# A 4 KB descriptor ring, one more place in five buffers, and two mixer norms moved in a decoder step's program

## The chip, the cores and the metric

The kernel runs on one core of a Trainium2 chip. A core has five engines that run side by side, each with its own queue of instructions: TensorE (PE, matrix products; PEld is its weight load), VectorE (DVE), ScalarE (ACT), GpSimd (POOL) and SyncE (SP, which here only starts transfers). They meet through semaphores. Transfers between the memory of the chip and the core's SBUF run on 16 DMA engines and are started from SP's, ACT's and POOL's queues. The metric is the device time of one execution in microseconds.

## The reference

One layer of a decoder for 512 prompt tokens and 8 x 8 sample tokens, width 2048, in float32.

```python
mod = (silu(c) @ w_ada + b_ada).reshape(-1, 6, D)        # shift1, scale1, gate1, shift2, scale2, gate2
h = rmsnorm(x) * (1 + scale1) + shift1
x_lru, y_gate, sc_b, sc_c, sc_x = split(h @ w_in)        # five groups of 1024 columns
out_lru = rglru(conv4(x_lru)) * gelu(y_gate)             # a recurrence over the tokens
out_sc = sc_b * conv3(sc_c * sc_x)
x = x + gate1 * (concat([rmsnorm(out_lru), rmsnorm(out_sc)]) @ w_out)
h2 = rmsnorm(x) * (1 + scale2) + shift2
# PEER: 8 heads, each takes the 16 best of 128 x 128 experts for each token
act = gelu(h2 . u[e]) * softmax(score)                   # for each token and chosen expert e
x = x + gate2 * sum(act * v[e])
y = rmsnorm(x)
```

Beside y, the last states of the recurrence and of both convolutions are returned. The inputs scale some of the norm weights and biases up.

## The kernel before

Products are made to float32 accuracy from three reduced ones: each operand is split into a high part (ACT's cast) and a low part (a subtraction on POOL or DVE), and TensorE adds high x high, low x high and high x low. A block of weights therefore passes SP's load (`raw`), ACT (`hi`), POOL (`lo`) and TensorE, in that order, through a few rotating places.

**Phase 1** (to about 960 us) has all 576 tokens in the free dimension. The order of TensorE's work is the order of the program text; that of the other engines is the scheduler's. The modulation is 96 pieces of 1 MB of `w_ada`, loaded into the pool `adap` (line 161). 32 of them run at the start; the other 64 stand in the list `todo` (line 349) and are put between the projections by `ada_turn(n, keep=7)` (line 351), which issues at most n pieces, stops at the end of a group of four, and leaves `keep` of them in the list. Lines 553 to 570 project and run the recurrence, eight tiles of 128 channels; lines 574 to 588 the short convolution, three projections (c, s, b) for each of eight tiles with `ada_turn(2)` behind each. `norm_stats` (line 224) puts a sum of squares through TensorE and takes a reciprocal root on DVE; the function that it returns, `spread` (line 232), has TensorE copy the root to all partitions and ACT copy that out to a buffer `R`. The recurrence's output is scaled by it inside the first short-conv tile (lines 578 to 586). The short convolution's is scaled at lines 597 to 604, between the first halves of the first two output tiles (`out_half`) and their second halves. Behind the output projection come gate, residual, second norm and queries.

**Phase 2** has two long stages in a hand-written order for all engines (line 985). Blocks of 128 experts with one first key are ranked by how many tokens choose them. The L = 80 first are computed densely, for all 512 prompt tokens, by products with whole blocks of u and v. The rest, and all sample tokens, are fetched as rows: a gather on POOL (`take`, line 1202) brings one expert's row for each of 128 partitions, and DVE multiplies and sums it.

- **U stage**, lines 1611 to 1682, 160 half-blocks n: `ahead` (line 910) loads and converts u's blocks, `u_half` (line 1363) runs 24 matmuls. Between them go the gate weights of the dense blocks, four tokens at a time: `g_pair` (DVE builds one-hots), `g_scale` (ACT scales them), `g_mm` (TensorE, into one PSUM bank) and `g_out` (ACT copies the bank to `stg`). `gm` holds how many groups have been built, multiplied and scaled. `LAG` holds the multiplication back by so many half-blocks, `PAIRS` bounds how many groups stand between building and multiplying, and PAIRS // 2 is the number of their buffers. The gathered rows of u go through `RB` places (`new_row`, line 827), fetched RB - 1 ahead (line 1304).
- **V stage**, lines 1722 to 1752, 80 steps m of two 512 KB blocks of v: `ahead(n + 7, n + 3)` loads seven blocks ahead and converts three ahead. `v_column` (line 1381) runs 12 matmuls for one of four PSUM banks, and `v_sum` (line 1410) adds a finished bank to the result on DVE, which frees it. The rows of v go through `RV` places, fetched RV - 2 ahead. Raw blocks have four places: two in the pool `ws`, one in `wx`, one in `vx`, taken in turn by `load` (line 880).

DVE and POOL serve several of these at once, in order: POOL holds the gathers and the subtractions in one queue, DVE the row products, the one-hots and the sums.

Of the kernel before, what the change touches and what calls it, by code (L numbers as in the profile page):

```python
# [39 lines left out]
SORTED = ((0, 64, 34), (64, 128, 47), (192, 128, 37), (320, 128, 30), (448, 64, 11))  # L40
RB = 4
RV = 6
ENDS = 5
# [6 lines left out]
FULL_ROWS = 1.25  # L50
LAG = 3
FIRST_G = 6
PAIRS = 6
EARLY_V = 16
# [26 lines left out]
def build(ctx, tc, A, O, dbg=None):  # L81
    nc = tc.nc
# [77 lines left out]
    big = p1.enter_context(tc.tile_pool(name="big", bufs=1))  # L160
    adap = p1.enter_context(tc.tile_pool(name="adap", bufs=3))
    wk = p1.enter_context(tc.tile_pool(name="wk", bufs=1))
# [188 lines left out]
    def ada_turn(n, keep=7):  # L351

        for a in pend:
            ada_out(*a)
        pend.clear()
        for _ in range(min(n, len(todo) - keep)):
            a = todo.pop(0)
            ada_mm(*a)
            if a[2] == 3:
                pend.append(a[:2])  # L360
                break
# [212 lines left out]
    for i in range(KW):  # L574
        sc_c(i, project(A["w_in"][24 + i], f"c{i}") if i else pc0)
        ada_turn(2)
        sc_x(i, project(A["w_in"][32 + i], f"s{i}"))
        if i == 0:
            spread = norm_stats(st, W, "g0")
        ada_turn(2)  # L580
        if i == 0:
            R = spread()
            st = []
            for k in range(KW):
                V.scalar_tensor_tensor(o[:, k, :], o[:, k, :], cols[:, C_GN + k:C_GN + k + 1], R, op0=ALU.mult, op1=ALU.mult)
        sc_b(i, project(A["w_in"][16 + i], f"b{i}"))
        ada_turn(2)
        square_sum(o[:, KW + i, :], i, st, "g1")
# [9 lines left out]
    spread = norm_stats(st, W, "g1")  # L598
    out_half(1, 0)
    ada_turn(2)  # L600
    R = spread()
    for k in range(KW, KD):
# [32 lines left out]
    R = spread()  # L635
# [244 lines left out]
    def load(n):  # L880
        if n >= len(stream):
            return
        s = stream[n]
        k = n % 3 if n < NU2 + 2 else (n - NU2 - 2) % 4
        pool, b = (ws, 2) if k < 2 else (wx, 1) if k == 2 else (pools["vx"], 1)
        raw = pool.tile([128, 8, 128], F32, name=f"raw{n}", tag="wraw", bufs=b)
# [710 lines left out]
    R1 = R2 = None  # L1597
    gm = [0, 0, 0, 0]
    ep = None
# [11 lines left out]
    for n in range(NU2):  # L1611
# [7 lines left out]
        if R1 is not None:  # L1619
# [8 lines left out]
            while gm[2] < gm[3]:  # L1628
                g_scale(gm[2])
                gm[2] += 1  # L1630
            gm[3] = gm[0]

# [89 lines left out]
    for m in range(M):  # L1722
        gi, q, bl, first, final = steps[m]
        n = NU2 + 2 * m
        ahead(n + 3, n + 3)
        ahead(n + 7, n + 3)
        if m == last:
# [181 lines left out]
```

## Time and profile before

| | |
|---|---|
| timed runs | 3267.7, 3271.77, 3271.31 us, median 3271.31 |
| profiled execution | 3275.15 us, its span 3273.3 us |
| granted TensorE clock, mean | 0.976 |
| moved by DMA | 882.84 MB |
| first matmul with u, first with v | about 1201 and 2262 us |

The timed runs differ by 0.12%. The profile is of one execution, 3.84 us above the median. Its page gives busy time for each engine, a chain of the work that ended last, and groups of instructions by line. Windows give the same for stretches of the span, waits say which engine stood idle and what ended the idle time, and a timeline lists instructions in order. A row of a timeline has start, length, engine, line, operation, the tiles written and read, and in brackets the idle time before it with what ended it. A row of waits has the total, how many times, and the longest.

### The profile page before, as it was taken

To read this page: it belongs to the slowest core of one execution; us is meant where nothing else is said; L and a number is where in the kernel's file an instruction comes from. 1 tells how busy PE (TensorE), PEld (TensorE's weight loads), DVE (VectorE), ACT (ScalarE), POOL (GpSimd) and SP (SyncE) were. 2 spreads that over 40 slices of the span, in tenths; PEclk is the share of its full clock that TensorE was granted. 3 is DMA by queue.
4 is the path that set the end of the run, shared out by engine and by line. 5 is a ranking of instruction groups with operands and counts; after the bars stand their busy time and mean duration, and the time that the engine had idled before them with its cause. 6 is when DMAs were issued, how large, how long until landed. Compare 5 with 4: busy or idle time off the path is not lost.

```text
span 3273.3 us, 46692 instructions
## 1 busy us (share of the span) xinstructions
PE 3088.6 (94%) x17239; PEld 2616.8 (80%) x17239; DVE 2173.3 (66%) x3265; ACT 1056.9 (32%) x1645; POOL 1718.4 (52%) x1000
## 2 busy tenths in 40 slices
PE   5999999999989999999999998998999999989897
PEld 2788898889979998887788787886888777777686
DVE  3465521142246898897998979856777787978755
ACT  3244311132232222222665555542222121122122
POOL 2233233344343335666556655656777676777742
PEclk9999999999989999999999999998999999999998
DMA  9744466634342228989779898989999988998964
GB/s 375 266 144 136 163 221 203 214 99 146 131 140 67 72 90 277 308 310 381 312 297 405 340 369 315 395 285 385 389 372 387 391 327 315 344 365 305 369 218 163
DMA packets 297067, 882.84 MB, mean 270 GB/s; under 512 B 37590, under 2 KB 79446, under 8 KB 245366
## 3 DMA queue, kind: packets, MB, share of 16 engines
q1 hardware_dynamic: 160608, 380.39, 33.3%
q0 software_dynamic: 66336, 413.41, 32.1%
q10 hardware_dynamic: 69888, 86.00, 7.5%
q8 instruction: 136, 2.23, 0.3%
q14 instruction: 99, 0.81, 0.1%
HBM read 879.89 MB, written 66.81 MB: 289 GB/s over the span
## 4 chain that ended last, share of the span: by engine, by line
PE 67%; DMA 15%; DVE 7%; issue 4%; POOL 4%; ACT 2%; ACTq 0%; SPq 0%; POOLq 0%; DVEq 0%
PE pu L1373 19%; PE pv L1393 14%; PE pp_o L139 6%; DMA v<-v,rows 4%; DMA gsb<-gd 4%; PE pp_c L139 3%; PE pp_s L139 3%; PE qa L139 3%; PE pp_b L139 3%; PE qb L139 3%; PE gbank L1573 2%; PE pp_x L139 2%; PE pp_y L139 2%; PE ada L189 2%; POOL xlo L905 2%
## 5 line engine op out<-in xcount | busy, mean ns | idle before, releaser
L905 POOL TENSOR_TENSOR xlo<-raw,xhi 128x1024 fp32r<-128x1024 f32 x320 | 785.6, 2467 | 453.8 <-ACT xhi L904 440.5
L904 ACT ACTIVATE xhi<-raw 128x1024 fp32r<-128x1024 f32 x320 | 338.2, 1060 | 868.6 <-PE pv L1393 353.6
L1258 DVE SCALAR_TENSOR_TENSOR accB<-v,dots,accB 128x2048 f32<-128x2048 f32 x211 | 496.3, 2352 | 159.4 <-DMA v<-v,rows 154.0
L1231 DVE SCALAR_TENSOR_TENSOR u<-u,hT 128x2048 f32<-128x2048 f32 x223 | 505.0, 2282 | 145.1 <-DMA u<-u,rows 130.2
L1393 PE MATMUL pv<-ahi,xhi 128*128 128x512 f32 x1280 | 514.8, 402 | 43.7 <-DVE acc L1415 33.7
L1393 PE MATMUL pv<-ahi,xlo 128*128 128x512 f32 x1280 | 510.8, 399 | 10.7 <-POOL xlo L905 10.5
L1373 PE MATMUL pu<-hhi,xhi 128*128 128x512 f32 x1280 | 516.9, 404 | 1.6 <-ACT xhi L904 1.6
L1373 PE MATMUL pu<-hhi,xlo 128*128 128x512 f32 x1280 | 504.7, 394 | 6.5 <-POOL xlo L905 6.5
L1393 PE MATMUL pv<-alo,xhi 128*128 128x512 f32 x1280 | 507.7, 397 | 0.0
L1373 PE MATMUL pu<-hlo,xhi 128*128 128x512 f32 x1280 | 506.0, 395 | 0.0
L1203 POOL DMA_INDIRECT u<-u,rows x223 | 227.6, 1021 | 207.1 <-DVE u L1231 155.2
L1393 PEld LDWEIGHTS pv<-ahi,xhi 128*128 128x128 f32 x1280 | 244.3, 191 | 107.8 <-DVE acc L1415 24.8
L1393 PEld LDWEIGHTS pv<-ahi,xlo 128*128 128x128 f32 x1280 | 244.1, 191 | 72.1 <-POOL xlo L905 15.1
L1203 POOL DMA_INDIRECT v<-v,rows x223 | 260.4, 1168 | 77.9 <-issue 36.3
L1373 PEld LDWEIGHTS pu<-hhi,xlo 128*128 128x128 f32 x1280 | 242.7, 190 | 61.7 <-POOL xlo L905 7.4
L1393 PEld LDWEIGHTS pv<-alo,xhi 128*128 128x128 f32 x1280 | 244.6, 191 | 54.7
L1373 PEld LDWEIGHTS pu<-hhi,xhi 128*128 128x128 f32 x1280 | 243.3, 190 | 52.5 <-ACT xhi L904 2.1
L1373 PEld LDWEIGHTS pu<-hlo,xhi 128*128 128x128 f32 x1280 | 243.0, 190 | 47.8
L1567 ACT ACTIVATE op<-op,it 128x128 f32<-128x128 f32 x512 | 155.9, 389 | 82.5 <-DVE op L1559 82.5
L1573 PEld LDWEIGHTS gbank<-wr,op 128*128 128x128 f32 x1024 | 134.4, 193 | 42.5 <-ACT stg L1580 33.1
L1573 PE MATMUL gbank<-wr,op 128*128 128x80 f32 x1024 | 133.6, 274 | 25.7 <-ACT stg L1580 25.5
L128 POOL TENSOR_TENSOR wlo_q<-raw_q,whi_q 128x1024 fp32r<-128x1024 f32 x28 | 67.8, 2420 | 142.5 <-ACT whi_q L126 142.5
(481 smaller groups left out, 5452.2 us busy)
## 6 DMA issues: line engine op xcount, KB each, us to landing
wa<-w_ada SPq DMA_DIRECT2D x96, 1024.0 KB
raw<-ut SPq DMA_DIRECT2D x160, 512.0 KB
raw<-v SPq DMA_DIRECT2D x320, 256.0 KB
actd<-act ACTq DMA_DIRECT2D x80, 256.0 KB
gd<-stg ACTq DMA_DIRECT2D x64, 320.0 KB
gsb<-gd ACTq DMA_DIRECT2D x80, 256.0 KB
actr<-actd ACTq DMA_DIRECT2D x40, 512.0 KB
raw_o<-w_out SPq DMA_DIRECT2D x32, 512.0 KB
```

The source lines that it names most:

```text
L128: lo_engine(share).tensor_sub(lo, raw, r32(hi))
L139: PE.matmul(o, st, mv[pick](k), start=first, stop=last)
L189: PE.matmul(acc[32 * g:32 * g + 32, :], cpad[:, 4 * kq + g, :], w[:, g, :], start=kq == 0, stop=kq == 3)
L904: S.activation(hi, raw, AF.Copy)
L905: G.tensor_sub(lo, raw, r32(hi))
L1203: G.indirect_dma_start(out=out, out_offset=None, in_=src, in_offset=bass.IndirectOffsetOnAxis(ap=idx, axis=0), bounds_check=NE * 128 - 1, ...
L1231: V.scalar_tensor_tensor(r, r, 1.0, st["h"], op0=ALU.mult, op1=ALU.mult, accum_out=dots[i][:, j:j + 1])
L1258: V.scalar_tensor_tensor(st["a"], r, dots[i][:, j:j + 1], st["a"], op0=ALU.mult, op1=ALU.add)
L1373: PE.matmul(pu, st[:, kk, :], movA[mv](k), start=k == 0 and a == 0, stop=k == KD - 1 and a == 2)
L1393: PE.matmul(pv, st, mv, start=first and j == 0 and a == 0, stop=last and not end and j == SG - 1 and a == 2)
L1567: S.activation(ops[:, j0 + j, :], ops[:, j0 + j, :], AF.Copy, scale=it[2][:, b * 4 + j:b * 4 + j + 1])
L1573: PE.matmul(pg[:, j * L:(j + 1) * L], ops[:, j0 + j, :], wr[:, j0 + j, :], start=True, stop=True)
```

## The change

[...] LAG grows by one and the list `gm` by one entry, so that a group is scaled one half-block later than before. In phase 1 the first `spread` is called behind the projection of the b tile and DVE's scalings behind `sc_b`; the second is called ahead of `ada_turn(2)`, and a second `ada_turn(2)` follows.

```diff
-RB = 4
-RV = 6
+RB = 5
+RV = 7
-LAG = 3
+LAG = 4
-PAIRS = 6
+PAIRS = 8
-    adap = p1.enter_context(tc.tile_pool(name="adap", bufs=3))
+    adap = p1.enter_context(tc.tile_pool(name="adap", bufs=4))
...
         ada_turn(2)
+        pb_ = project(A["w_in"][16 + i], f"b{i}")
         if i == 0:
             R = spread()
             st = []
+        sc_b(i, pb_)
+        if i == 0:
             for k in range(KW):
                 V.scalar_tensor_tensor(o[:, k, :], o[:, k, :], cols[:, C_GN + k:C_GN + k + 1], R, op0=ALU.mult, op1=ALU.mult)
-        sc_b(i, project(A["w_in"][16 + i], f"b{i}"))
         ada_turn(2)
...
     out_half(1, 0)
+    R = spread()
     ada_turn(2)
-    R = spread()
+    ada_turn(2)
     for k in range(KW, KD):
...
-        k = n % 3 if n < NU2 + 2 else (n - NU2 - 2) % 4
-        pool, b = (ws, 2) if k < 2 else (wx, 1) if k == 2 else (pools["vx"], 1)
+        k = n % 3 if n < NU2 + 2 else (n - NU2 - 2) % 5
+        pool, b = (ws, 2) if k < 2 else (wx, 1) if k == 2 else (pools["vx"], 2)
...
-    gm = [0, 0, 0, 0]
+    gm = [0, 0, 0, 0, 0]
...
-            gm[3] = gm[0]
+            gm[3], gm[4] = gm[4], gm[0]
...
-        ahead(n + 7, n + 3)
+        ahead(n + 8, n + 3)
...
-    nc = _bacc.Bacc("TRN2", target_bir_lowering=False, num_devices=1)
+    nc = _bacc.Bacc("TRN2", target_bir_lowering=False, num_devices=1, dynamic_dma_scratch_size=4096)
```

## The prediction

> **What bounds the kernel now.** I read the page first, then the windows, then the waits, then the timeline of the places that the change touches. The page:
>
> ```profile
> PE 3088.6 (94%) x17239; PEld 2616.8 (80%) x17239; DVE 2173.3 (66%) x3265; ACT 1056.9 (32%) x1645; POOL 1718.4 (52%) x1000
> PE 67%; DMA 15%; DVE 7%; issue 4%; POOL 4%; ACT 2%; ACTq 0%; SPq 0%; POOLq 0%; DVEq 0%
> ```
>
> TensorE is busy 94% of the span and holds 67% of the chain that ended last. No edit takes a matmul away, so only time that TensorE loses can be won. The busy share hides part of that time, because matmuls that follow a stall run slower. I therefore count matmuls. The next three rows are 25 us windows of TensorE alone; their columns are length, busy time (instructions), granted clock, DMA share, GB/s.
>
> ```profile
> 2350.00:2375.00 25.00, 25.00 (x110) 1.00 1.04 394
> 2575.00:2600.00 25.00, 19.47 (x70) 0.86 0.95 359
> 2075.00:2100.00 25.00, 25.00 (x135) 1.00 1.02 424
> ```
>
> Undisturbed, the V stage starts 110 matmuls in 25 us (4.4 per us); the U stage, with the small gate matmuls between, 135 (5.4 per us). The window at 2575 lost 40 matmuls, 9.1 us, although only 5.5 us of it were idle. With these rates I price whole stretches (all engines: PE, PEld, DVE, ACT, POOL, then clock, DMA share, GB/s):
>
> ```profile
> 0.00:135.00 135.00, 95.61 (x613) 54.42 (x613) 46.65 (x108) 40.96 (x67) 37.52 (x37) 0.91 0.96 357
> 1600.00:1850.00 250.00, 238.96 (x1239) 200.42 (x1238) 221.44 (x289) 148.50 (x323) 150.97 (x104) 0.99 0.93 372
> 1850.00:2100.00 250.00, 236.12 (x1217) 199.88 (x1216) 216.06 (x275) 143.53 (x312) 146.12 (x100) 0.97 0.88 340
> 2275.00:2575.00 300.00, 299.02 (x1289) 242.39 (x1287) 222.59 (x128) 73.46 (x74) 209.13 (x123) 1.00 1.01 385
> 2575.00:2875.00 300.00, 277.54 (x1152) 220.56 (x1152) 243.55 (x138) 63.21 (x58) 210.73 (x127) 0.97 0.90 338
> 2875.00:3175.00 300.00, 277.78 (x1178) 221.76 (x1179) 221.13 (x137) 64.05 (x59) 200.65 (x117) 0.98 0.85 309
> ```
>
> U loses (1350 - 1239)/5.4 = 20.6 us and (1350 - 1217)/5.4 = 24.6 us in its two rows, 45 us. V loses (1320 - 1289)/4.4 = 7, then 38 and 32 us: 77 us, 70 of them after 2575. What TensorE waited for, over the whole run:
>
> ```profile
> PE ada L189 <- DMA wa<-w_ada: 36.4, 15, 18.2
> PE pv L1393 <- DVE acc L1415: 33.7, 18, 4.9
> PE gbank L1573 <- ACT stg L1580: 25.5, 15, 5.6
> ACT op L1567 <- DVE op L1559: 82.5, 37, 11.5
> ```
>
> **V stage: one more row place, fetch depth 4 to 5, one more raw place.** One disturbance, POOL, ACT and DVE timelines merged in order of time:
>
> ```profile
> 2571.87 1.06 ACT L904 ACTIVATE xhi<-raw 128x1024 fp32r<-128x1024 f32 x1 [12.92 <-DMA raw<-v]
> 2573.02 4.15 POOL L905 TENSOR_TENSOR xlo<-raw,xhi 128x1024 fp32r<-128x1024 f32 x1 [7.73 <-ACT xhi L904]
> 2580.67 1.00 POOL L1203 DMA_INDIRECT v<-v,rows  x1
> 2589.33 2.36 DVE L1258 SCALAR_TENSOR_TENSOR accB<-v,dots,accB 128x2048 f32<-128x2048 f32 x1 [9.72 <-DMA v<-v,rows]
> ```
>
> A raw block is late, ACT waits 12.92 us, POOL waits behind ACT, the gathers queued behind POOL's subtraction go out late, and DVE then waits 9.72 us for a row. DVE's sums (L1415) free TensorE's PSUM banks, so TensorE stops too: that is the 33.7 us above. The waits of 2575 to 3175 alone, and the gathers of 2275 to 3180:
>
> ```profile
> ACT xhi L904 <- DMA raw<-v: 115.6, 27, 21.2
> DVE accB L1258 <- DMA v<-v,rows: 78.9, 38, 10.0
> L1203 POOL DMA_INDIRECT v<-v,rows x207: 987/998/3089, 2274.0 to 3126.8; - x104
> ```
>
> A mean row wait is 78.9/38 = 2.1 us, a mean raw wait 115.6/27 = 4.3 us. One more row of lead is 852.8/207 = 4.1 us; one more raw block is 24 matmuls, 24/4.4 = 5.5 us. So each added place is worth more than the mean wait it stands against, less than the longest (10.0 and 21.2). The bounds: nothing, if the transfers simply end later; at most 70 us after 2575. DMA leaves room for it: (0.90 + 0.85) x 300 = 525 us of DMA work at the share of 1.01 that the row of 2275 holds is 520 us, and TensorE needs (1152 + 1178)/4.4 = 530 us for these 600. But both floors are nearly equal, and in stretches where DMA is full an added place is used once and not refilled, so I take 40% of the 70: **28 us** (range 10 to 50).
>
> **U stage: fifth row, LAG 4, PAIRS 8, the scale one half-block later.** The gate bank is one PSUM bank: TensorE's next group waits until ACT has copied it out (25.5 us in 15 waits). ACT is late because its scaling of the one-hots stands in its queue ahead of the copy and waits for DVE: 82.5 us in 37 waits, 2.2 us each, longest 11.5. The longer gm list moves each scaling one half-block back, which is 24 + 16 matmuls, 40/5.4 = 7.4 us. That covers all but the longest of these waits. LAG and PAIRS keep the matmul one step and one buffer behind, so nothing is taken back. What is not covered is ACT's wait at a change of token group:
>
> ```profile
> L1218 ACT ACTIVATE hT<-h2r 128x2048 f32<-128x2048 f32 x5 | 9.5, 1903 | 13.3 <-DVE u L1231 12.1 <-DMA h2r<-h2d,tok 1.2
> ```
>
> Of the 94.6 us that ACT waits for DVE (82.5 + 12.1), 87% go, so 22 of the 25.5; DVE itself is busy 216 to 221 us of 250 and catches up slowly, so I take not quite two thirds of that, **14 us**, between nothing and the 45 counted. The fifth row shortens DVE's waits for rows, but as the window at 2075 shows a DMA share of 1.02 in this stage I add nothing for it. The last gate group moves one step later. Its stores must land before ACT loads them, in ACT's own queue, ahead of the casts:
>
> ```profile
> 2165.41 0.76 ACT L1580 ACTIVATE stg<-gbank 128x320 f32<-128x320 f32 x1 [2.91 <-issue]
> 2191.47 1.17 ACTq L1324 DMA_DIRECT2D gsb<-gd  x2
> ```
>
> There are 26 us between the last copy and the first load; one step of 7.4 us fits. Cost nothing, and if the cover went it would be at most those 7.4.
>
> **First mixers' norm.** TensorE's timeline, two pieces of the chain, and what the other engines do around it:
>
> ```profile
> 369.75 1.92 PE L189 MATMUL ada<-wa,cpad 128*32 128x512 f32 x16
> 375.37 1.13 PE L236 MATMUL st_g<-ident,rc_g 128*128 128x128 f32 x8 [3.70 <-DVE rc_g L149]
> 376.74 14.31 PE pp_b L139 x96
> 393.34 12.98 PE pp_c L139 x96
> 369.76 2.37 POOL L128 TENSOR_TENSOR wlo_b<-raw_b,whi_b 128x1024 fp32r<-128x1024 f32 x1 [4.00 <-ACT whi_b L126]
> 377.29 5.92 DVE L585 SCALAR_TENSOR_TENSOR o<-o,cols,R_g 128x576 f32<-128x576 f32 x8 [2.06 <-ACT R_g L240]
> 392.07 0.69 ACT L216 ACTIVATE sqa_g<-o 128x576 f32<-128x576 f32 x1
> 399.73 1.06 ACT L126 ACTIVATE whi_s<-raw_s 128x1024 fp32r<-128x1024 f32 x1 [6.98 <-PE pp_c L139]
> ```
>
> The spread waits 3.70 us for DVE's reciprocal root, and the projection behind it runs 14.31 instead of 12.98 us. Behind the projection the root has long been ready, and the projection's weights are converted at 372.1, half a tile ahead of their use. Saved: 3.70 + 1.33 = **5.0 us**. What becomes late: DVE's eight scalings (5.92 us) now follow sc_b; ACT's first square, which writes the buffer that they read, waits for them, near 392 as before; the next cast in ACT's queue is due at 399.7, so about 6 us of cover remain. If the cover went, TensorE would give back at most the 5.92.
>
> **Second mixers' norm.** The list of modulation pieces is held back at 7 (line 351's keep). 64 pieces go out one or two per call, and the seventh-last is reached in the third call of the seventh short-conv tile. From there the calls at this place find nothing. The row of L189 alone shows it, with no piece between 664 and 732; the wait stands behind it:
>
> ```profile
> 664.00:732.00 68.00, 0.00 (x0) 0.95 0.29 96
> 717.29 0.33 PE L238 MATMUL st_g<-ident,rc_g 128*128 128x64 f32 x2
> 721.23 0.85 PE L139 MATMUL pp_o<-hhi,whi_o 128*128 128x288 f32 x2 [3.61 <-ACT hhi L245]
> ```
>
> So the four pieces that the spread is put ahead of are empty, and the order stays as it is: **0 us**; were they real, 3.61 us.
>
> **Fourth modulation buffer and the moved addresses.** In the first 135 us DMA's share is 0.96, so a deeper queue brings no byte sooner; the 36.4 us stay: 0. Everything in SBUF lies elsewhere, and phase 2's fifth row is cleared on POOL while phase 1 still drains:
>
> ```profile
> L840 POOL MEMSET row<- x4: 1803/1810/1812, 958.9 to 964.2; 128x2048 f32 x4
> 976.48 5.84 DMA h2d<-h2s
> ```
>
> A fifth clearing is 1.8 us on an idle POOL. If its address waited for the h2 stores, POOL would stand from 966 to 982, and the next weights with it: 0 to 16 us. I take 0 and keep 16 for the range.
>
> **The ring.** The gathers' median of 998 ns (row above) is one issue; if the smaller ring never fills it stays, and the cost is 0. [...]
>
> **Sum.** 28 + 14 + 5 = 47 us from the profiled execution's 3275.15 us (its span is 3273.3) gives 3228. The median of the timed runs, 3271.31, lies 3.8 below the profiled one, so the time I name is 3271.31 - 47 = **3224 us**.
>
> **The rivals.** (1) *The places fill once and the stages stay bound by bandwidth.* For it: shares of 1.02 to 1.04 in the 25 us rows. Against it: 0.85 and 0.90 after 2575, where the loss is. V then gives 6, U 4, the norm 5: 3256 us.
>
> (2) *Slower: gathers crowd out the raw blocks in V.* The queues:
>
> ```profile
> q1 hardware_dynamic: 160608, 380.39, 33.3%
> q0 software_dynamic: 66336, 413.41, 32.1%
> ```
>
> A gather packet has 413.41 MB/66336 = 6.2 KB, a packet of SP's queue 2.4 KB. If the queues take turns by packet, a burst that is one row longer (1.05 MB, 2.7 us at 385 GB/s) holds raw blocks back by that much. 27 raw waits x 2.7 = 73 us more on ACT; today's 115.6 + 78.9 us of waits go with 70 us of lost TensorE time, 0.36 each, so 26 us. U has the fifth row too and the same two queues, so its 14 us go as well, and only the norm's 5 stay: 3271 + 26 - 5 = 3292 us. It decides once the added delay exceeds the 5.5 us of the fifth raw place, which speaks against it. [...]
>
> (3) *The ring is the new wait.* If it held fewer than the five rows asked for, gathers would queue on POOL ahead of its subtractions: one row of lead lost, 38 x 4.1 x 0.36 = 56 us: 3310 us. Against it: bursts of four are issued now without a pause.
>
> (4) *The second norm does what it says*: 3220 us; excluded by the row of L189.
>
> **Chances.** Forecast 0.60, its own range 3190 to 3248, with 0.02 of it lost to the moved addresses and within 0.2%; rival 1 0.25, of it 0.08 within 0.2%; rival 2 0.10; rival 3 0.05; rival 4 none. About 0.2%, 6.5 us, is what a measurement of this kernel can tell from no change. Faster 0.58 + 0.17 = 0.75, same 0.10, slower 0.15. The range 3190 to 3276 leaves out rivals 2 and 3 and the forecast's lower edge; it takes in the 16 us of the moved addresses.
>
> **What would show it.** Right: TensorE's wait at pv for DVE below 20 us, gbank's below 10, ACT's for DVE's one-hots below 20, no gap ahead of the first norm's spread, the gap near 717 unchanged, gathers still at 1.0 us. Wrong: raw waits above 115.6 after 2575 (rival 2), gathers longer than 1.0 us in the median (rival 3), DMA share at 1.01 with the same loss (rival 1), or a new POOL wait near 965.

## The result and the profile after

| | before | after |
|---|---|---|
| timed runs, median (8 each) | 3272.84 us | 3251.56 us (3243.18 to 3262.13) |
| ratio, 95% interval | | 0.9933 (0.9912 to 0.9953) |
| profiled execution (span) | 3275.15 (3273.3) us | 3251.38 (3249.6) us |

The change gains 21.3 us (15 to 29 by the interval), where 47 were forecast. Two runs of the experiments below, one of 6058 us (v_back) and one of 4309 us (norm_only), count as slow, and the ratios leave them out. The page of the kernel after:

```profile
PE 3082.5 (95%) x17239; PEld 2617.8 (81%) x17239; DVE 2195.8 (68%) x3265; ACT 1052.3 (32%) x1645; POOL 1713.7 (53%) x1001
PE 75%; DMA 12%; DVE 5%; issue 5%; POOL 2%; ACT 1%; SPq 0%; ACTq 0%; POOLq 0%; DVEq 0%
```

TensorE holds more of the chain of work that ended last (75% for 67%). The two long stages are read from the groups of TensorE's matmuls by tile: count, shortest, median and longest duration in ns, then the start of the first and the last. Before:

```profile
L1373 PE MATMUL pu<-hhi,xhi x1280: 387/393/774, 1200.5 to 2261.8; 128*128 128x512 f32 x183
L1393 PE MATMUL pv<-ahi,xhi x1280: 387/393/793, 2262.5 to 3247.3; 128*128 128x512 f32 x183
```

After:

```profile
L1376 PE MATMUL pu<-hhi,xhi x1280: 387/393/774, 1191.2 to 2242.2; 128*128 128x512 f32 x183
L1396 PE MATMUL pv<-ahi,xhi x1280: 387/393/794, 2242.9 to 3223.9; 128*128 128x512 f32 x183
```

Phase 2 starts 9.3 us earlier, the U stage is 10.3 us shorter (1051.0 for 1061.3), the V stage 3.8 (981.0 for 984.8). The lengths that follow and those in the expectations go to the very last matmul of a stage, 0.4 us more in U and 1.5 in V: U 1061.7 before and 1051.5 after, V 986.3 and 982.5. So the term of 28 us for V is the one that is missing. The windows of V, as in the prediction:

```profile
2275.00:2575.00 300.00, 292.18 (x1253) 235.50 (x1252) 225.35 (x128) 72.22 (x69) 209.40 (x122) 0.99 0.99 377
2575.00:2875.00 300.00, 275.58 (x1145) 219.85 (x1145) 253.35 (x138) 61.68 (x56) 208.42 (x127) 0.97 0.90 335
2875.00:3175.00 300.00, 283.05 (x1223) 228.18 (x1222) 227.44 (x142) 63.33 (x60) 193.29 (x110) 0.98 0.85 310
```

V loses (1320 - 1253)/4.4 = 15 us, then 40 and 22: 77 us, as before (7, 38, 32). The first window is worse, the last better. After's V starts 19.6 us earlier; with the windows moved by as much it starts 1271, 1148 and 1205 matmuls, 3624 in all where before starts 3619, so the loss is the same there too. What TensorE and DVE wait for, over the whole run of after, and DVE's waits in its V stage (2243 to 3175):

```profile
PE pv L1396 <- DVE acc L1418: 40.1, 15, 6.0
PE gbank L1576 <- ACT stg L1583: 25.4, 4, 13.6
```

```profile
DVE accB L1261 <- DMA v<-v,rows: 46.5, 28, 4.0
DVE actr L1339 <- DMA actr<-actd: 43.5, 6, 13.4
DVE actr L1339 <- DMA raw<-v: 20.2, 2, 14.8
```

Before, in the same stage (2263 to 3195):

```profile
DVE accB L1258 <- DMA v<-v,rows: 134.2, 64, 10.0
DVE actr L1336 <- DMA raw<-v: 13.3, 3, 7.3
DVE actr L1336 <- DMA actr<-actd: 9.5, 3, 4.3
```

The row waits went as the prediction meant them to, 134.2 to 46.5. But TensorE's wait for DVE's sums doesn't fall with them: it is 40.1 us for 33.7. (That is no rise either: three profiles without V's places have 33.7 to 42.2 us, eight with them and the same gate weights' layout 30.0 to 40.1.) What grew is DVE's wait at the weighing (`weigh`, the product of a group's activations `actr` with its gate weights `gsb`), 22.8 to 63.7 us. The name behind the arrow is the load that landed last by the profile, and for the 20.2 it is a raw block, which the weighing doesn't read; what it does read are `actr` and `gsb`. One such place, DVE's timeline, then TensorE's, then ACT's:

```profile
2610.64 3.54 DVE L1339 TENSOR_TENSOR actr<-actr,gsb 128x2048 f32<-128x2048 f32 x1 [8.85 <-DMA actr<-actd]
2614.10 7.12 DVE L1261 SCALAR_TENSOR_TENSOR accB<-v,dots,accB 128x2048 f32<-128x2048 f32 x3
2623.08 2.35 DVE L1261 SCALAR_TENSOR_TENSOR accB<-v,dots,accB 128x2048 f32<-128x2048 f32 x1 [1.86 <-DMA v<-v,rows]
2625.35 1.28 DVE L1418 TENSOR_TENSOR acc<-acc,pv 128x512 f32<-128x512 f32 x2
```

```profile
2626.18 0.77 PE L1396 MATMUL pv<-ahi,xhi 128*128 128x512 f32 x1 [4.58 <-DVE acc L1418]
```

```profile
2605.61 0.34 ACTq L1334 DMA_DIRECT2D actr<-actd  x1
2606.13 2.01 ACT L907 ACTIVATE xhi<-raw 128x1024 fp32r<-128x1024 f32 x2 [17.48 <-DMA actr<-actd]
```

DVE stands 8.85 us for the activations, works off the rows that have piled up meanwhile, reaches the sum of a finished bank at 2625, and TensorE has waited 4.58 us for that bank. The second half of `actr` goes out only at 2605.61, behind 17.48 us in which ACT stood. Both `gsb` and `actr` have one buffer (`bufs=1`), so a group's loads can start only when the group before has been weighed; a second buffer was not tried. The loads that it stands for, with their median time to landing (KB of one, us):

```profile
raw<-v SPq DMA_DIRECT2D x320, 256.0 KB, 7.4
gsb<-gd ACTq DMA_DIRECT2D x80, 256.0 KB, 16.5
actr<-actd ACTq DMA_DIRECT2D x40, 512.0 KB, 14.3
```

The same 256 KB take 16.5 us as `gsb` on ACT's queue, in pieces of 512 bytes (4 blocks x 32 tokens x 4 bytes), and 7.4 as a raw block on SP's, in pieces of 2 KB. That small pieces make the loads late is the theory the experiments start from, against two others: bandwidth as such, and a loss elsewhere (addresses, ring) that eats a real gain.

### The profile page after: what moved, and what is told of

Same layout as the page of the kernel before. It is cut to its first block, busy times and chain, and to the rows that moved or that the text cites. A ratio compares the mean times of both kernels' runs of the same rounds, so it can differ in the third digit from the quotient of the medians.

```text
span 3249.6 us, 46645 instructions
## 1 busy us (share of the span) xinstructions
PE 3082.5 (95%) x17239; PEld 2617.8 (81%) x17239; DVE 2195.8 (68%) x3265; ACT 1052.3 (32%) x1645; POOL 1713.7 (53%) x1001
## 3 DMA queue, kind: packets, MB, share of 16 engines
q0 software_dynamic: 66336, 413.41, 32.3%
## 4 chain that ended last, share of the span: by engine, by line
PE 75%; DMA 12%; DVE 5%; issue 5%; POOL 2%; ACT 1%; SPq 0%; ACTq 0%; POOLq 0%; DVEq 0%
PE pu L1376 24%; PE pv L1396 16%; PE pp_o L139 6%; DMA v<-v,rows 3%; PE pp_c L139 3%; PE pp_s L139 3%; PE gbank L1576 3%; PE qa L139 3%; PE pp_b L139 3%; PE qb L139 3%; PE ada L189 2%; PE pp_x L139 2%; PE pp_y L139 2%; DMA gsb<-gd 2%; DMA actr<-actd 2%
## 5 line engine op out<-in xcount | busy, mean ns | idle before, releaser
L1234 DVE SCALAR_TENSOR_TENSOR u<-u,hT 128x2048 f32<-128x2048 f32 x223 | 505.0, 2282 | 128.6 <-DMA u<-u,rows 126.1
L1396 PE MATMUL pv<-ahi,xhi 128*128 128x512 f32 x1280 | 514.6, 402 | 43.1 <-DVE acc L1418 40.1
L1206 POOL DMA_INDIRECT u<-u,rows x223 | 224.9, 1009 | 154.8 <-DVE u L1234 94.4
L1576 PEld LDWEIGHTS gbank<-wr,op 128*128 128x128 f32 x1024 | 136.3, 195 | 38.0 <-ACT stg L1583 27.5
L1576 PE MATMUL gbank<-wr,op 128*128 128x80 f32 x1024 | 133.1, 274 | 25.4 <-ACT stg L1583 25.4
L1418 DVE TENSOR_TENSOR acc<-acc,pv 128x512 f32<-128x512 f32 x144 | 96.7, 681 | 65.4 <-PE pv L1396 65.2
## 6 DMA issues: line engine op xcount, KB each, us to landing
gsb<-gd ACTq DMA_DIRECT2D x80, 256.0 KB, 16.5
actr<-actd ACTq DMA_DIRECT2D x40, 512.0 KB, 14.3
```

The source lines that it names most:

```text
L1206: G.indirect_dma_start(out=out, out_offset=None, in_=src, in_offset=bass.IndirectOffsetOnAxis(ap=idx, axis=0), bounds_check=NE * 128 - 1, ...
L1234: V.scalar_tensor_tensor(r, r, 1.0, st["h"], op0=ALU.mult, op1=ALU.mult, accum_out=dots[i][:, j:j + 1])
L1396: PE.matmul(pv, st, mv, start=first and j == 0 and a == 0, stop=last and not end and j == SG - 1 and a == 2)
L1418: V.tensor_add(ak, ak, pv)
L1576: PE.matmul(pg[:, j * L:(j + 1) * L], ops[:, j0 + j, :], wr[:, j0 + j, :], start=True, stop=True)
```

## The experiments

Times are medians, ratios are to the kernel before on the same chip; U and V are stage lengths from the profile.

### One part at a time

**v_back**: the V stage's places taken back.

```diff
-RV = 7
+RV = 6
-        k = n % 3 if n < NU2 + 2 else (n - NU2 - 2) % 5
-        pool, b = (ws, 2) if k < 2 else (wx, 1) if k == 2 else (pools["vx"], 2)
+        k = n % 3 if n < NU2 + 2 else (n - NU2 - 2) % 4
+        pool, b = (ws, 2) if k < 2 else (wx, 1) if k == 2 else (pools["vx"], 1)
-        ahead(n + 8, n + 3)
+        ahead(n + 7, n + 3)
```

> The changed kernel with the V stage as it was before: RV 6, one raw place in vx, blocks loaded seven ahead. The rest of the change stays. Theory A (the V places removed row waits that did not end last, and were worth the 4 us by which the V stage got shorter): V stage 984 to 987 us long, time 3252 to 3258 us, 15 to 21 below the kernel before. Rival B (the places are worth the 28 us of the forecast, and something else of the change, such as the moved addresses or the smaller ring, took 24 of them away): the V stage is 1000 us or longer, time 3270 us or more. Rival C (the places themselves do harm and good that cancel, because the deeper gather bursts crowd the loads on ACT's queue): V stage as in theory A, and DVE's waits for actr and gsb at the weighing fall from 63.7 back to about 23 us.

3248.43 us, 0.9916 (0.9898 to 0.9933); U 1045.7, V 989.5. Rival B falls: without the places the time is the same. DVE's row waits are back at 129.9 us, and its waits at the weighing fall to 26.9, as rival C had it (V is 2.5 us longer than expected, less than V moves from profile to profile):

```profile
DVE actr L1339 <- DMA raw<-v: 16.1, 2, 10.7
DVE actr L1339 <- DMA actr<-actd: 10.8, 3, 5.0
```

So the deeper fetch takes 83 us of row waits from DVE and adds 37 at the weighing, while TensorE's wait for DVE's sums is 42.2 us here and 40.1 in after. The waits at the weighing hold over the profiles: 23 to 27 us in three without the places, 55 to 83 in eight with them.

**u_back**: the gate groups as before.

```diff
-LAG = 4
+LAG = 3
-PAIRS = 8
+PAIRS = 6
-            gm[3], gm[4] = gm[4], gm[0]
+            gm[3] = gm[0]
```

> The changed kernel with LAG 3, PAIRS 6 and the scaling one half-block earlier, as before; the fifth row place (RB 5), the V stage and phase 1 stay changed. Theory (the gate groups' order is what made the U stage 10 us shorter): the U stage from its first to its last matmul goes from 1051.5 back to 1058 to 1062 us, ACT's waits for DVE's one-hots go from 7.0 back to 70 or more, time 7 to 11 us above the changed kernel. Rival (the fifth row place did it): U stage stays within 2 us of 1051.5, time within 3 us of the changed kernel, though ACT's waits return.

3249.96 us, 0.9923 (0.9903 to 0.9942); U 1049.2. The theory fails. ACT's waits for the one-hots come back in part (47.3 us, where 70 or more were expected), and TensorE's for the gate bank do not change with them. Groups of ACT in after and in u_back, then TensorE's wait in u_back:

```profile
L1570 ACT ACTIVATE op<-op,it 128x128 f32<-128x128 f32 x512 | 154.4, 388 | 7.2 <-DVE op L1562 7.0
```

```profile
L1570 ACT ACTIVATE op<-op,it 128x128 f32<-128x128 f32 x512 | 155.2, 388 | 47.3 <-DVE op L1562 47.3
```

```profile
PE gbank L1576 <- ACT stg L1583: 21.6, 8, 5.1
```

With the change the same 25 us stand in four waits of up to 13.6 us instead of fifteen. The longest of them is behind one row of ACT in after:

```profile
1872.48 1.88 ACT L1221 ACTIVATE hT<-h2r 128x2048 f32<-128x2048 f32 x1 [17.38 <-DVE u L1234]
```

ACT's copy of the next tokens' h waits until DVE has done the old tokens' products, 17.38 us, and the copy of the gate bank stands behind it. In all, ACT waits 21.4 us for DVE at this copy in after, 11.6 in u_back and 12.1 before.

**rb4**: the fifth row place of U taken back, all else changed. **after_again**: the changed kernel beside it.

```diff
-RB = 5
+RB = 4
```

> The changed kernel with RB 4, four row places in the U stage as before; RV stays 7, LAG, PAIRS and the later scaling stay changed. Theory R (the fifth row place, which the prediction priced at nothing, made the U stage shorter, and the later scaling did not): the U stage, 1049 to 1052 us with five places, comes to 1058 to 1063, DVE's waits for rows of u rise, and the time is 8 to 14 us above the changed kernel. Rival L (the list and LAG did it, and the run with the list undone kept its U stage by chance): U stage 1047 to 1053, time within 4 us of the changed kernel.

> The changed kernel as it is, beside the others on the same chip, for the spread of one kernel from profile to profile: the V stage within 4 us of 982.5, the U stage within 5 us of 1051.5, time 3245 to 3256 us. If the stages differ by more than that, single profiles can't tell the parts of the change apart.

rb4 3267.76 us, 0.9980 (0.9965 to 0.9994), U 1065.3; after_again 3249.87 us, 0.9927 (0.9906 to 0.9949), U 1042.0, V 989.9. The fifth place is worth 17.9 us. Over all profiles with the gate weights' layout of before, U is 1061.7, 1063.5 and 1065.3 with four places and 1042.0 to 1051.5 (mean 1046.6 of nine) with five: 17 us. The changed kernel's own U and V move by 9.5 and 7.4 us between its two profiles, more than I had allowed for, so single stage lengths don't tell 5 us. DVE's waits for rows of u are 134.2 us in rb4, 126.1 and 112.1 in the two profiles of the changed kernel. What the place removes most is POOL's wait in front of a gather, which holds the subtractions queued behind it; rb4, then after:

```profile
POOL u L1206 <- DVE u L1234: 147.5, 98, 10.8
```

```profile
POOL u L1206 <- DVE u L1234: 94.4, 71, 4.3
```

**norm_only**: the kernel before with the first norm's edit alone.

```diff
+        pb_ = project(A["w_in"][16 + i], f"b{i}")
         if i == 0:
             R = spread()
             st = []
+        sc_b(i, pb_)
+        if i == 0:
             for k in range(KW):
...
-        sc_b(i, project(A["w_in"][16 + i], f"b{i}"))
```

> The kernel before with one edit: the first mixers' spread behind the projection of the b tile, and the scalings behind the product with it. By the sum of the prediction 5.0 us are saved: the gap of 3.70 us ahead of the spread is gone, the projection behind it takes 13.0 instead of 14.3 us, and phase 1 ends 5 us earlier; time 3265 to 3269 us where the kernel before is at 3272. Rival (the 5 us are given back, since phase 2 is bound by loads which start no earlier): phase 1 ends 5 us earlier and the time stays within 1 us.

3266.30 us, 0.9974 (0.9957 to 0.9991). From the norm's sums to the output projection 327.8 us for 333.2: 5.4 us. TensorE's timeline in after; no wait is left:

```profile
366.51 1.17 PE L228 MATMUL pc_g<-ones,sqa_g 128*128 128x1 f32 x10
367.61 1.92 PE L189 MATMUL ada<-wa,cpad 128*32 128x512 f32 x16
369.46 0.53 PE L139 MATMUL pp_b<-hhi,whi_b 128*128 128x288 f32 x2
```

**adap3**: the fourth modulation buffer taken back.

```diff
-    adap = p1.enter_context(tc.tile_pool(name="adap", bufs=4))
+    adap = p1.enter_context(tc.tile_pool(name="adap", bufs=3))
```

> The changed kernel with three buffers for the modulation pieces, as before. If the fourth buffer is what shortened TensorE's waits for them (35 us in two kernels with three, 27 to 30 in six with four): the waits come back to about 35 us, and the first norm's sum is 3 to 6 us later than the 365 to 367 us of the kernels with four. If it was worth nothing, as predicted: waits below 30 us, that sum at 364 to 367 us.

One run, 3250.46 us. TensorE's wait, and with it the norm's sums at 368.4 us:

```profile
PE ada L189 <- DMA wa<-w_ada: 35.5, 14, 18.5
```

It is 27.5 in after. Over all profiles the sums stand at 364.3 to 367.8 us with four buffers (mean 366.2 of 17) and at 368.4 to 371.9 with three (mean 369.6 of three): about 3 us.

**acts_early** issues the loads of `actr` two columns earlier:

```diff
-            jobs.setdefault(max(hi_at + 6 + 2 * q, 0), []).append(lambda sg=sg, q=q: load_acts(sg, q))
+            jobs.setdefault(max(hi_at + 4 + 2 * q, 0), []).append(lambda sg=sg, q=q: load_acts(sg, q))
```

> The changed kernel with the two loads of each set of activations (actr) issued two columns, about 5.5 us, earlier in the V stage; nothing else. Theory A (the V stage now waits in DVE's weighing, which stands ahead of the sums that free TensorE's banks, for loads that take 14 us to land and are issued 11 us ahead): DVE's waits at the weighing fall from 63.7 to 25 us or less, the V stage gets 5 to 20 us shorter, time 3232 to 3247 us. Rival D (DMA bandwidth is the bound of the V stage; each removed wait comes back at another place): waits at the weighing fall but row waits or raw waits rise by as much, V stage within 3 us, time 3249 to 3254 us.

3248.42 us, 0.9915 (0.9895 to 0.9936); V 984.8, the wait at the weighing for `actr` 62.7 instead of 43.5; all waits there are 78.1 us, within the 64 to 82 of the changed kernel's two profiles. So theory A's cure fails. The median from issue to landing is 17.5 us, for 14.3 and 11.1 in those two. The loads stand in ACT's queue behind those of `gsb`; that this is the reason was not shown here.

### What V waits for

**thin_rows** leaves seven eighths of each gathered row of v out, and DVE's sums read the rest eight times over; **no_gsb** leaves out the loads of the gate weights after the third group, and DVE weighs with the third group's again. Only the lines for the loads are shown.

```diff
-            take(held[j][0], A["v"], rows_i[i][:, j:j + 1])
+            take(held[j][0][:, :256], A["v"].rearrange("e (a c) -> (e a) c", a=8), rows_i[i][:, j:j + 1])
...
```

```diff
+        if sg > 2:
+            return
         nc.scalar.dma_start(gsb[sg][:, c, :], gd[c, :, sg * SG:(sg + 1) * SG, :].rearrange("c p i t -> p c (i t)"))
...
```

> The changed kernel with the gathers of the V stage carrying an eighth of each row (256 columns of 2048, at other rows), and DVE's sums reading these columns eight times over: the same instructions with 180 MB less moved. Theory B (DMA bandwidth bounds the V stage): 180 MB at 385 GB/s are 470 us of DMA; the waits of ACT for raw blocks (152 us) and of DVE for rows and actr fall below 20 us each and the V stage falls from 982 to 900 us or less. Theory Q (the stage is bound by the order of DVE's and ACT's own work): raw and row waits fall, the V stage stays above 950 us.

> The changed kernel without the loads of the gate weights (gsb) behind the third group of four blocks: 17 MB in packets of 512 bytes on ACT's queue are left out, and DVE weighs with the third group's weights again and again. Theory P (small packets on ACT's queue make the activations late, and DVE's weighing holds up everything behind it): DVE's waits at the weighing fall from 63.7 to under 10 us and the V stage gets 20 us shorter or more. Theory B (bandwidth): 17 MB at 385 GB/s are 44 us of DMA at most, of which a share like that of the other removed waits comes through: the V stage 5 to 20 us shorter, with row or raw waits about as before.

One run each. thin_rows: 3170.36 us, V 907.2, no wait of TensorE for DVE's sums left, and `gsb` lands in 3.6 us instead of 16.5. no_gsb: 3198.89 us, V 940.6: 18 MB less give 42 to 49 us, as theory P had it, more than twice what theory B allowed. Two windows of no_gsb, then the first of thin_rows:

```profile
2275.00:2575.00 300.00, 300.00 (x1302) 244.24 (x1301) 238.36 (x135) 75.17 (x71) 218.68 (x129) 1.00 0.98 374
2575.00:2875.00 300.00, 300.00 (x1303) 244.27 (x1302) 264.83 (x153) 70.24 (x63) 229.48 (x140) 1.00 0.91 352
2275.00:2575.00 300.00, 300.00 (x1303) 244.27 (x1302) 241.30 (x139) 70.33 (x65) 219.52 (x129) 1.00 0.57 180
```

DMA is as full as in after (0.98 and 0.91 for 0.99 and 0.90), and TensorE starts 1302 and 1303 matmuls instead of 1253 and 1145, as many as thin_rows with a DMA share of 0.57. So here DMA engines at a share of 0.98 didn't by themselves stop TensorE. This run by itself doesn't exclude a stage that is paced by its bytes: 18 MB are 6% of the 307 MB that after's three windows moved, and V is 4 to 5% shorter. The runs of the next section, with the same bytes, do. Why both cures work, the page's queues of after say (packets, MB, share of 16 engines' span):

```profile
q0 software_dynamic: 66336, 413.41, 32.3%
q1 hardware_dynamic: 160608, 380.39, 33.0%
q10 hardware_dynamic: 69888, 86.00, 7.4%
```

A packet is what the trace's packet records list one by one: in after 512 bytes for `gsb` (40960 of them on ACT's queue), 2 KB for a raw block of v and 8 KB for a gathered row (50314 on the gathers' queue). On the mean, with packets of 4 bytes counted in, a packet of the gathers' queue takes 0.323 x 3249.6 x 16/66336 = 0.25 us of an engine, one of SP's 0.11, one of ACT's (q10) 0.055. If the three take turns, ACT's queue gets one packet in 0.42 us where all have work. The packet records of after agree with turns: from 2566 to 2590 us, while `gsb` is on its way, 978 rows of 8 KB start on the gathers' queue, 1077 pieces of 512 bytes on ACT's and 603 blocks of 2 KB on SP's; from 2576 to 2580 alone, with packets of 4 bytes counted in, 168, 167 and 165. So in these 24 us a piece of 512 bytes came only 1.1 times as often as a row 16 times its size, and an engine gets to one of ACT's in 24 x 16/1077 = 0.36 us. V's loads of `gsb` are 80 x 256 KB/512 = 40960 packets, 2560 for each engine: by this estimate some 910 us at that pace, nearly the whole stage. By this reading thin rows shorten the turn (`gsb` lands in 3.6 us), missing gate weights the queue (12 loads of `gsb` are left of 80). How many pieces one turn takes the counts don't show.

### The same bytes in larger packets

**gd_layout** stores the gate weights by group of four blocks; V's loads then run over 2 KB of one partition, U's stores over 512 bytes. **gd_vback** is the same with v_back's edit.

```diff
-    gd = dr.tile([NCH, 128, L, TC], F32, name="gd")
+    gd = dr.tile([L // SG, 128, NCH, SG * TC], F32, name="gd")
-        nc.scalar.dma_start(gsb[sg][:, c, :], gd[c, :, sg * SG:(sg + 1) * SG, :].rearrange("c p i t -> p c (i t)"))
+        nc.scalar.dma_start(gsb[sg][:, c, :], gd[sg][:, c, :])
-                puts.append(lambda q=q: nc.scalar.dma_start(gd[c][:, q:q + L // 4, :], full[:, q:q + L // 4, :]))
+                puts.append(lambda q=q: nc.scalar.dma_start(gd[q // SG:(q + L // 4) // SG, :, c, :].rearrange("s p x -> p s x"), full[:, q:q + L // 4, :].rearrange("p (s i) t -> p s (i t)", i=SG)))
```

> The changed kernel with the gate weights laid out in memory by group of four blocks, so that V's loads of gsb go in packets of 2 KB instead of 512 bytes; the same bytes, and the U stage's stores go in 512 bytes instead of 2.5 KB. Leaving these loads out altogether made the V stage 42 to 49 us shorter. Theory P (the loads are late because their small packets take turns with 8 KB rows and 2 KB blocks): gsb lands in 6 to 10 us instead of 16.5, DVE's waits at the weighing fall below 30 us, the V stage comes to 945 to 970 us, time 3215 to 3238 us. Theory B (the 17 MB themselves are the cost): V stage within 5 us of 982 to 990, time 3245 to 3256. Against a gain: the stores of U, 41 thousand small packets there, could make the U stage up to 10 us longer.

> The kernel of the new layout of the gate weights, with the V stage's places as they were before (RV 6, one raw place in vx, seven blocks ahead). If the places of the change were only hidden behind the late gate weights, they are worth more now: the V stage is 10 to 28 us longer than with the new layout alone. If TensorE never waited for what they bring, the two V stages agree within 5 us, as they do with the old layout (989.5 against 982.5 and 989.9).

gd_layout 3279.24 us, 1.0005 (0.9987 to 1.0024): V 954.7, U 1119.8. gd_vback 3279.17 us, 1.0019 (1.0004 to 1.0035): V 965.2, U 1108.8. V gains what theory P says, with the same bytes, and U loses more than that, far over the 10 us allowed. V is 10.5 us longer in gd_vback than in gd_layout, the lower edge of what had been expected. The stores' issues on ACT in gd_layout (count, shortest, median, longest in ns), and TensorE's wait:

```profile
L1588 ACTq DMA_DIRECT2D gd<-stg x64: 366/680/14105, 1589.6 to 2230.6; - x64
PE gbank L1576 <- ACT stg L1583: 70.6, 17, 15.4
```

An issue takes up to 14.1 us of ACT (1.24 at most in after), and the gate bank's copies stand behind. In V it is the other way round; the issues of `gsb` in after and in gd_layout:

```profile
L1327 ACTq DMA_DIRECT2D gsb<-gd x80: 366/377/9791, 2174.3 to 3067.8; - x80
L1327 ACTq DMA_DIRECT2D gsb<-gd x80: 326/327/698, 2250.9 to 3110.5; - x80
```

With those of `actr`, 16 issues over 1 us hold ACT for 58 us in after, and one of 1.05 us is left in gd_layout. So part of V's gain may come from ACT, which is no longer held, and not from DVE's earlier weights; the runs don't part the two.

**gd_one** puts fewer stores at a time, **gd_sp** does that and issues them from SP:

```diff
-            put(2)
+            put(1)
-            for q in range(0, L, L // 4):
+            for q in range(0, L, L // 5):
-                puts.append(lambda q=q: nc.scalar.dma_start(
+                puts.append(lambda q=q: nc.sync.dma_start(
...
```

> The new layout of the gate weights, with the U stage's stores in five parts of 16 blocks instead of four of 20, and one part issued per half-block instead of two. The new layout alone made V 28 to 35 us shorter and U 68 to 78 us longer, with issues of these stores that take up to 14.1 us on ACT. Theory S (ACT is held while a second store's small packets find no room behind the first): issues of 1 us or less, TensorE's waits for the gate bank fall from 70.6 to about 25, the U stage comes back to 1042 to 1058 us, the V stage stays at 950 to 960; time 3215 to 3235. Rival (the stores' bytes in 512-byte packets hold up the rows and blocks whatever their spacing): U stage 1080 us or longer, time 3250 or more.

> The same, with these stores issued from SP's queue in place of ACT's. Theory S: ACT is never held, the U stage is 1040 to 1052 us, the V stage 950 to 960, time 3210 to 3230. Rival (SP's queue is held instead, and u's blocks come late): TensorE waits for xhi and xlo at pu in U, the U stage is 1070 us or longer.

gd_one 3337.43 us, 1.0202 (1.0172 to 1.0231), U 1162.5: theory S is wrong there. Its stores' median issue is down to 0.37 us, but they land so late that the buffer `stg` isn't free. Who waited for these stores:

```profile
  ACT stg L1583: 104.3, 9
```

gd_sp 3221.44 us, 0.9848 (0.9819 to 0.9877): U 1058.2, V 945.9. So it is the queue, not the spacing: the same 512-byte stores among SP's blocks cost 7 to 16 us of U (predicted none), on ACT's queue 57 to 120. Turns alone don't tell the two queues apart: by the packet records the 40960 small pieces go out within 654 us from ACT's queue in gd_layout, 696 in gd_one and 592 from SP's in gd_sp. gd_layout loses at the issues (108 us of ACT in those over 1 us), gd_one at the landing (104.3 us for `stg`); gd_sp has 36 us, on SP, and 15.5. Why the stores land sooner from SP's queue stays open. V's windows:

```profile
2275.00:2575.00 300.00, 300.00 (x1303) 244.25 (x1302) 234.43 (x134) 76.03 (x74) 213.69 (x124) 1.00 1.00 394
2575.00:2875.00 300.00, 288.81 (x1231) 232.43 (x1230) 257.11 (x146) 65.32 (x60) 221.33 (x136) 0.99 0.93 359
```

At a DMA share of 1.00 and 394 GB/s TensorE starts 1303 matmuls, as many as in thin_rows, where after starts 1253, and then 1231 where after starts 1145. **gd_sp_vback** takes V's places back here:

> The kernel with the new layout and the stores on SP's queue (3221 us, V stage 946), with the V stage's places as before the change (RV 6, one raw place in vx, seven blocks ahead). With the old layout the places changed nothing in the time and 3 us in the V stage on the mean of seven and three profiles; with the new layout one pair of profiles differs by 10.5 us. If the late gate weights hid the places' worth: V stage 955 to 965 us, time 3230 to 3240. If the places are worth nothing in either: V stage 942 to 950, time 3216 to 3227.

3235.35 us, 0.9883 (0.9863 to 0.9902), V 965.7, 20 us longer than in gd_sp. By the medians it is 14 us slower, by the ratios 11, and the intervals of the two ratios overlap a little; against gd_sp_norm2 below, on the same chip, it is 17 us slower, and those intervals don't overlap. v_back had cost nothing. So the places are worth some 11 to 14 us once the gate weights are in time, and at most a few while they are late.

### Further gains

**rb6r** adds a sixth row place (RB 6) with the gate groups of u_back, which leave the room, and a ring of 2048 bytes (the setting `dynamic_dma_scratch_size`). **gd_sp_rb6** is the same on gd_sp.

```diff
-RB = 5
+RB = 6
-    nc = _bacc.Bacc("TRN2", target_bir_lowering=False, num_devices=1, dynamic_dma_scratch_size=4096)
+    nc = _bacc.Bacc("TRN2", target_bir_lowering=False, num_devices=1, dynamic_dma_scratch_size=2048)
```

> The changed kernel with a sixth row place in the U stage (RB 6), the gate groups' order as before (LAG 3, PAIRS 6), which frees the space, and a ring of 2048 bytes instead of 4096. Theory R (rows' places bound POOL's queue in U; the fifth was worth 15 to 18 us): POOL's waits for DVE to free a place fall from 94 to 50 to 70 us, the U stage gets 3 to 10 us shorter than 1042 to 1051, time 3240 to 3248. Rival (the fifth place was enough): within 4 us of 3250. Ring: a place for a descriptor is short if the gathers' median rises above 1.0 us; I expect 1.0.

> The stores on SP's queue, and with it the sixth row place in U, the gate groups' order as before, and the ring of 2048 bytes. The sixth place took 9 us off the changed kernel's time. If both gains add up: 9 us below the kernel with the stores on SP's queue, 3200 to 3220, faster than the kernel before and the changed one. If the new stores and the sixth row's gathers collide: no better than the kernel with the stores on SP's queue.

rb6r 3240.96 us, 0.9892 (0.9871 to 0.9913), U 1039.4: 9 us below the changed kernel, the intervals touch. gd_sp_rb6 3233.44 us, 0.9885 (0.9854 to 0.9917), U 1068.5: they don't add up, it is 12 us slower than gd_sp. Whether its rows collide with the stores or the older gate order tells there stays open. The gathers with 2048 bytes of ring, and with 4096 in after:

```profile
L1206 POOL DMA_INDIRECT v<-v,rows x223: 985/996/3022, 2162.8 to 3079.4; - x112
```

```profile
L1206 POOL DMA_INDIRECT v<-v,rows x223: 985/996/2986, 2169.4 to 3089.6; - x112
```

**norm2** holds eleven modulation pieces back, so that four stand behind the second spread; **gd_sp_norm2** is the same on gd_sp.

```diff
-    def ada_turn(n, keep=7):
+    def ada_turn(n, keep=11):
     R = spread()
-    ada_turn(2)
-    ada_turn(2)
+    ada_turn(2, 7)
+    ada_turn(2, 7)
```

> The changed kernel with eleven modulation pieces held back in place of seven, and two calls of two pieces behind the second spread that may take them down to seven, so that the four pieces of the change's name are there. By the prediction's rival 4 the gap of 3.9 us ahead of the first matmul behind the spread goes, and from the first matmul of the output projection to the first with u it takes 3 to 4 us less than 497, the pieces' own time (4 x 1.9 us) being moved in and out of this stretch as well: they are added here, so the stretch would read 497 - 3.6 + 7.7 = 501 and the one before it 327.8 - 7.7 = 320. Time 3246 to 3252. Rival: the gap stays, since ACT's copy of R is late for another reason; the two stretches add up to 824.6 as now.

> The kernel with the new layout and the stores on SP's queue, and with it the eleven modulation pieces held back, of which four then stand behind the second spread. Those shortened the gap there from 3.9 to 0.95 us. Both together: 3 us below the kernel without them, 3214 to 3222, the fastest of all. If phase 2 waits for loads that start no earlier: within 1 us of it, which this measurement can't tell from the first case by the time, only by the place of the first matmul with u.

In after the place is as it was, in norm2 the pieces (x24) cover it:

```profile
709.82 0.33 PE L238 MATMUL st_g<-ident,rc_g 128*128 128x64 f32 x2
713.76 0.53 PE L139 MATMUL pp_o<-hhi,whi_o 128*128 128x288 f32 x2 [3.61 <-ACT hhi L245]
```

```profile
704.55 2.78 PE L189 MATMUL ada<-wa,cpad 128*32 128x512 f32 x24
708.27 0.53 PE L139 MATMUL pp_o<-hhi,whi_o 128*128 128x288 f32 x2 [0.95 <-ACT hhi L245]
```

The two stretches add up to 822.1 us for 824.6 (323.4 and 498.7; the expected split of 320 and 501 was off). One run, 3250.52 us, can't show 2.5. gd_sp_norm2 has 3218.69 us, 0.9837 (0.9816 to 0.9858), the lowest of all, 1.0% below the changed kernel; it is not told apart from gd_sp.

## Why the prediction was right or wrong

**V stage, 28 us: wrong; the step is the 40% of 70 us.** It let each added place remove TensorE's loss because it removed waits of DVE and ACT. The waits went (rows 134.2 to 46.5; raw waits after 2575 from 115.6 to 96.5), the loss stayed at 77 us. Undone, the places change the time by nothing; on the mean of eight and three profiles V is 984.8 with them and 988.9 without, 4 us. (The 70 were a little too large themselves: 1320 matmuls come from one window of 25 us, and thin_rows starts 1303 in 300 us at full work. By that rate V lost 67 us before and 66 after.) The path went through another load of the same engine: `gsb` and `actr`, behind which DVE weighs, which come later with the places (26.9 us of waits without them, 63.7 with), and which I had in no row of the working. Removing the loads of `gsb` (42 to 49 us of V) or making them quicker (28 to 44) took most of the loss away, and then the places were worth 11 to 14.

**U stage, 14 us: the size is near, the reason wrong.** The step "of the 94.6 us that ACT waits 87% go, so 22 of the 25.5" failed at the "so": the waits went (82.5 to 7.0), and the gate bank's 25.5 stayed at 25.4. Its longest part stands behind ACT's copy of h, whose wait I had named as not covered, with 12.1 us, and which is 21.4 in after. List, LAG and PAIRS are worth nothing. The fifth row place, priced at nothing because of a DMA share of 1.02, is worth 17 to 18 us: it shortens POOL's wait in front of a gather (147.5 us in rb4, 94.4 in after), and POOL's subtractions stand behind that. By how much TensorE's gain goes through these subtractions was not shown apart. Its waits for the gate bank are 25.5 to 33.1 us in the three profiles with four places and 21.6 to 25.4 in the nine with five, some 5 of the 17 us on the mean.

**First norm, 5.0 us: right**, 5.4 in the stretch. **Second norm, 0: right**, the gap is 3.9 us in both. **Ring, 0: right**, gathers at 996 ns for 998; how far the ring fills no run shows. **Moved addresses, 0: right in the time**, but the wait that I priced at 0 to 16 us, and named as a sign, is there. In all profiles with five row places or more POOL stands some 7 us until the h2 stores land, and it doesn't with four (before, rb4):

```profile
974.70 8.98 POOL L843 MEMSET row<- 128x2048 f32 x5 [7.36 <-DMA h2d<-h2s]
```

From 950 to 1000 us TensorE waits 0.7 us for weights that POOL makes, and the first matmul with u is 9.3 us earlier than before.

**Fourth modulation buffer, 0: mis-sized**, about 3 us; its longest wait, 18.3 us, is the same, some of the shorter ones are gone (15 to 9).

So the 21 us are, from the runs, about 17 from the fifth row place, 5 from the norm, 3 from the modulation buffer and 0 to 4 from V; that sums to 25 to 29, the upper end of the interval of 15 to 29. Rival 1's time (3256) is near, its reason isn't: no_gsb has the same DMA share without the loss, and gd_sp a share of 1.00 with the same bytes. Rival 2 (gathers crowd out raw blocks) fell with the raw waits, though its mechanism was there at another load: the gathers crowded out the gate weights (`gsb` lands in 16.5 us, and in 3.6 with thin rows); rival 3 fell with the gathers' 996 ns (its 3310 doesn't follow from its terms: 3271 + 56 is 3327, and 3308 if the 14 and the 5 still come off), rival 4 with its empty calls. Of the signs that I named, TensorE's wait for DVE below 20 us (40.1) and the gate bank's below 10 (25.4) said at once which two steps had failed.

## What to carry to other kernels

Here DVE, which serves several streams in order, stood 134.2 us for rows before and 46.5 after, and at the weighing 22.8 and then 63.7: before pricing a place for one stream, list every load that the engine waits for, with its landing time, and ask which is late once this one isn't. A removed wait counts only if the wait behind it at the bottleneck goes too: ACT's for the one-hots went from 82.5 to 7.0 us, and TensorE's for the gate bank stayed at 25.4. Undoing one part at a time showed here that two terms of the sum had been given to the wrong edits. And look at packet sizes by queue: V's loads in 2 KB instead of 512 bytes, with U's stores moved to SP's queue, were worth 30 us by the medians (gd_sp 3221.44, after 3251.56), the added places 17, 3 and 0 to 4.

## What the runs showed of the hardware

- In after, loads of 256 KB land in 16.5 us (median) as `gsb` in 512-byte packets on ACT's queue and in 7.4 as raw blocks in 2 KB packets on SP's, in the same stage. At a DMA share of 0.98 (no_gsb) and 1.00 (gd_sp) TensorE starts 1302 and 1303 matmuls in 300 us, as many as at 0.57 (thin_rows).
- In 24 us of after (2566 to 2590) the gathers' queue and ACT's start pieces in nearly equal numbers, though the sizes differ by 16: 978 of 8 KB and 1077 of 512 bytes. With an eighth of each gathered row of v the 512-byte loads land in 3.6 us (thin_rows).
- One issue of a transfer in 512-byte pieces took up to 14.1 us of ACT (stores, gd_layout), 9.8 of ACT (loads of `gsb`, after) and 7.0 of SP (stores, gd_sp); in larger pieces the stores took 1.24 at most (2560 bytes, after) and the loads of `gsb` 0.70 (2 KB, gd_layout). The loads of `actr`, in 4 KB pieces on the same queue as `gsb`, took up to 9.6 in after. The same stores cost U 7 to 16 us from SP's queue (gd_sp) and 57 to 120 from ACT's (gd_layout, gd_vback, gd_one).
- With the setting `dynamic_dma_scratch_size` at 2048 (rb6r) and 4096 (after) the gathers' median is the same 996 ns.
- The changed kernel's U and V stages differ by 9.5 and 7.4 us between two profiles (after, after_again).
